# Five more places to yield in the recurrence streams of a hybrid layer, and two groups of copies in the other order

## The chip, the cores and the metric

One Trainium2 chip, one of its cores. The metric is device time in microseconds (us) of the whole launch. The engines are named as in the profile: PE (TensorE matmul) and PEld (its weight load), DVE (VectorE), ACT (ScalarE), POOL (GpSimd), SP (SyncE, which issues most transfers).

## The reference

One decoder layer on x of 2048 tokens and 1024 columns, float32. HGRN2 heads (four of 128) and RWKV-7 heads (eight of 64) run side by side on one input projection; one output projection and a ConvFFN follow.

```python
h = _rmsnorm(x, norm1_w[l])
proj = h @ w_in[l]
...
o_hg = _hgrn2_mixer(q_raw, f_raw, i_raw, g_raw, lower_bounds[l], hg_norm_w[l])
...
o_rw = _rwkv7_mixer(r, k, v, wd, ad, gd, rw_w0[l], rw_w2[l], rw_a0[l], rw_a2[l], rw_g2[l],
                    rw_k_k[l], rw_k_a[l], rw_r_k[l], rw_ln_w[l], rw_ln_b[l])
x = x + jnp.concatenate([o_hg, o_rw], axis=-1) @ w_out[l]
x = x + _conv_ffn(_rmsnorm(x, norm2_w[l]), w_up[l], conv_w[l], conv_b[l], w_down[l])
```

Inside the RWKV mixer the state follows S = S diag(w) + (S a) b^T + v k^T for each token, and y = S r. The kernel computes this by chunks of 64 tokens, which needs the inverse of a triangular 64 x 64 matrix for each chunk and head.

## The kernel before

The work has two stages. Stage 1 (to about 1350 us) makes the input projection, both mixers and the output projection; stage 2 is the ConvFFN and is not touched by the change. Stage 1 walks over four blocks of 512 tokens with three Python generators that emit instructions in turn:

- the dense stream: norm, turn, projection, and behind each block its output projection. Each float32 product is made of three matmuls of split operands (L265 to L267, with high and low halves that L242/L249 on ACT and L243/L250 on DVE make). `turn` (L436) transposes a block of x on PE, and eight ACT copies (xt) take the result from PSUM. The output projection of a block (L373 and below) loads pieces of w_out (woraw), splits them (L249, L250), multiplies, and adds the residual on DVE (L407).
- the RWKV stream, `rw_super`: eight steps, two for each block (each holds four of the eight heads). 
- the HGRN stream, `hg_unit`: sixteen units, four for each block, one head each.

The main loop at L1077 to L1086 advances the RWKV stream by one piece (up to its next `yield`), then the HGRN stream by one, then calls `fill(TICK)`, which advances the dense stream until pieces worth 2000 ns have been emitted. A `yield` in a mixer is therefore what puts dense matmuls between two dependent pieces of that mixer. A mixer that has to wait for its inputs yields `None` until the projection has made them. The emitted order is then set into an order for each engine by the framework, whose engines wait for each other by semaphores.

The pieces of one RWKV step that the change and the prediction speak of, in their order: KB and BV on DVE (L702); M from matmuls at L714; its blocks are copied out to E by a DMA; transposes and the copies UV and RHS on ACT (L120, the line of the helper `act`); lv at L763; the inverse of 32 x 32 blocks on DVE as 31 pairs L783 and L785, each reading what the one ahead wrote; TZ (L789), the transposed result; z at L802 and its ACT copy ZT; z2 at L815 and its ACT copy TTs; the product of the whole inverse with RHS at L828, whose result ACT copies to two places, M (three copies, the columns called Q) and UV (four copies). XH and xp follow: L848 reads UV and KBT, L862 reads M and KBT, and L865 and L868 on DVE take its results. Further down is a scan over eight chunks (L885, L887), L917 and the output copies.

One HGRN unit: hk at L926; transposed values VT; seven levels of scaling on DVE (L944 to L953) with matmuls at L969 and masks at L975; hk times Sf at L1004; the transposes KT at L1011, the state product at L1022 and its DVE scan (L1024); the norm of the output (osq) with matmul L1037; and L1042.

ACT's functions come from tables. `act` (L112 to L124) loads another table set where a function needs one that is not loaded (L116 in the profile): Exp and Ln share a set, Sigmoid and Tanh share one, Silu has its own; Copy, Square and Identity need none. So the number of loads depends on the order in which ACT's instructions are emitted.

Of the kernel before, what the change touches and what calls it, by code (L numbers as in the profile page):

```python
# [11 lines left out]
AF = mybir.ActivationFunctionType  # L12
# [52 lines left out]
def tile_layer(ctx, tc, consts, x, norm1_w, w_in, hg_lb_logits, hg_norm_w, rw_shift_mu, rw_w0, rw_w2,  # L65
# [46 lines left out]
    def act(out_, in_, func, **kw):  # L112

        want = tables.get(func)
        if want is not None and want != tab["now"]:
            pre = S.preload_act_table_set(want)  # L116
            for u_ in tab["uses"]:
                tc.add_manual_dep(pre.ins, u_.ins.name, NOSYNC, reason="table order")
            tab.update(now=want, pre=pre, uses=[])
        i_ = S.activation(out_, in_, func, **kw)  # L120
        if want is not None:
            tc.add_manual_dep(i_.ins, tab["pre"].ins.name, NOSYNC, reason="table order")
            tab["uses"].append(i_)
        return i_  # L124
# [144 lines left out]
    def phase1(c1):  # L269
# [354 lines left out]
        er0 = lambda e: 64 if e == 0 else 0  # L624

        def quads():

            return [(b, h, e, u) for b in range(4) for h in range(2) for e in range(2) for u in U]

        def col0(u, e):  # L630

            return er0(e) if u == 0 else 64 - er0(e)
# [5 lines left out]
        def rw_super(nb, s_):  # L638

            tl = stage[("tl", nb)]  # L640
            r, k, v = (stage.pop(("rkv", nb, s_, w)) for w in range(3))
            prs = (2 * s_, 2 * s_ + 1)
            pc = [slice(p * P, (p + 1) * P) for p in prs]

            def tile_(tag, shape, name):
                return rp.tile([P] + shape, F32, tag=tag, name=name)

            def bank2():
                return ps.tile([P, 2, BLK], F32, tag="rw", name="rw", bufs=2)
# [52 lines left out]
            V.tensor_mul(KB[:, :, 1:3, :], v16(c), v16(a))  # L702
            V.tensor_mul(BV, b1, v)
            yield

            M = tile_("M", [2, 2, 4, 2, P], "M")
            for j in range(2):
                for u in U:
                    s1 = bank2()
                    for i in range(4):  # L710
                        b, e = 2 * j + i // 2, i % 2
# [12 lines left out]
            for e in range(2):  # L724
                for q in range(2):
                    r0 = er0(e) + 32 * q
# [29 lines left out]
            act(RHS[0:64, :, :, 0:64], tpv[64:128], AF.Copy)  # L756
            done["rw1"] += 1
            yield

            lv = bank2()  # L760
            for b, h, e, u in quads():
                kr, c0, sl = 64 - er0(e), col0(u, e), (b * 2 + h) * 64
# [5 lines left out]
            for e in range(2):  # L768
                r0, c0 = er0(e), col0(1, e)
# [9 lines left out]
            for j in range(31):  # L779
# [6 lines left out]
                if j % 4 == 3:  # L786
                    yield
            TZ = tile_("XH", [16, 16, 2], "TZ")
            V.transpose(TZ.rearrange("p c m f -> p (c m f)"), Ti.rearrange("m t c -> m c t"))  # L789
            ZT = tile_("E", [16, 32], "ZT")  # L790
            TZm = TZ.rearrange("p c m f -> p m c f")
            for q in (1, 0):
                for e in range(2):
                    r0 = er0(e) + 32 * q
# [4 lines left out]
            for b, h, e, u in quads():  # L799
                r0 = er0(e)  # L800
                c0, sl = r0 + 32 - 32 * u, u * 256 + (b * 2 + h) * 32
                TE.matmul(z[c0:c0 + 32, 0, sl:sl + 32], M[r0:r0 + 32, e, u, b, h, 32:64],  # L802
                          TZm[r0:r0 + 32, u * 8 + b * 2 + h], start=True, stop=True, tile_position=(r0, c0))
            for u in U:
                for e in range(2):
                    r1 = er0(e) + 32
                    c0 = r1 - 32 * u
                    act(ZT[r1:r1 + 32, 8 * u:8 * u + 8],
                        z[c0:c0 + 32, 0, u * 256:u * 256 + 256].rearrange("p (s t) -> p s t", t=32), AF.Copy)
            yield  # L810
            z2 = bank2()
            for b, h, e, u in quads():
                r0 = er0(e)
                c0, sl = r0 + 32 * u, u * 256 + (b * 2 + h) * 32
# [3 lines left out]
            for u in U:  # L818
                for e in range(2):
                    r0 = er0(e)  # L820
                    c0 = r0 + 32 * u
# [4 lines left out]
            for b, h, e, u in quads():  # L826
                r0, c0, sl = er0(e), col0(u, e), ((b % 2) * 2 + h) * P
                TE.matmul(qus[u][c0:c0 + 64, b // 2, sl:sl + P], TTs[r0:r0 + 64, u * 8 + b * 2 + h, :],  # L828
                          RHS[r0:r0 + 64, 4 * u + b, h, :], start=True, stop=True, tile_position=(r0, c0))
            quv = [qus[u].rearrange("p j (b h t) -> p (j b) h t", h=2, t=P) for u in U]  # L830
            act(M[:, 0, 0, :, :, 0:64], quv[0][:, :, :, 0:64], AF.Copy)
            for e in range(2):
                r0, c0 = er0(e), col0(1, e)
                act(M[r0:r0 + 64, 0, 1, :, :, 0:64], quv[1][c0:c0 + 64, :, :, 0:64], AF.Copy)
            for u in U:
                for e in range(2):
                    r0, c0 = er0(e), col0(u, e)
                    act(UV[r0:r0 + 64, 4 * u:4 * u + 4, e, :].rearrange("p b (h t) -> p b h t", t=64),
                        quv[u][c0:c0 + 64, :, :, 64:128], AF.Copy)
            yield  # L840
            XH = tile_("XH", [2, 9, 64], "XH")
            V.tensor_copy(XH[:, :, 0, :], Xc[:, 2 * s_:2 * s_ + 2, :])
            xp = bank2()
            for u in U:
                for ch in range(8):
                    b, e = ch // 2, ch % 2
# [24 lines left out]
            for u in U:  # L871
                for ch in range(8):
                    b, e = ch // 2, ch % 2
# [5 lines left out]
            for ch in range(8):  # L879
                b, e = ch // 2, ch % 2  # L880
                cs_ = slice(ch * 64, ch * 64 + 64)
                for u in U:
                    for h in range(2):
                        hr = slice(h * 64, h * 64 + 64)
                        TE.matmul(xp[hr, u, cs_], M[hr, 1, u, b, e, 0:64], XH[hr, u, ch, :], start=False,  # L885
                                  stop=ch == 7, tile_position=(h * 64, h * 64), skip_group_check=True)
                V.tensor_mul(XH[:, :, ch + 1, :], xp[:, :, cs_], WC2[:, :, ch].broadcast_to([P, 2, 64]))  # L887
                yield
            V.tensor_copy(Xc[:, 2 * s_:2 * s_ + 2, :], XH[:, :, 8, :])
            for u in U:  # L890
                for ch in range(8):
                    cs_ = slice(ch * 64, ch * 64 + 64)
                    for h in range(2):
                        hr = slice(h * 64, h * 64 + 64)
                        TE.matmul(yp[hr, u, cs_], XH[hr, u, ch, :], RT[hr, u, ch, :], start=False, stop=ch == 7,
                                  tile_position=(h * 64, h * 64), skip_group_check=True)
# [26 lines left out]
        def hg_unit(nb, j):  # L923
# [79 lines left out]
            X = scaled(6)  # L1003
            V.tensor_mul(k, k, Sf)  # L1004
            V.tensor_mul(q, q, Pf)
            yield
            KT = rp.tile([P, 4, P], F32, tag="Sf", name="KT")
            tp = bank("hg")
            lp = bank("hg")
# [4 lines left out]
                          start=True, stop=True, tile_position=(0, 0))  # L1014
            act(KT, tp.rearrange("p (b t) -> p b t", t=P), AF.Copy)
            act(Af[0:64, :, 64:128], lp[0:64, 0:256].rearrange("p (b t) -> p b t", t=64), AF.Copy)
            yield
            SH = rp.tile([P, 5, P], F32, tag="SH", name="SH")
            V.tensor_copy(SH[:, 0, :], Sc[:, j, :])
            sps = bank("hg")  # L1020
# [26 lines left out]
        def rw_stream():  # L1047
            for n in range(2 * NBLK):
                while ready["rw"] <= n:
                    yield None  # L1050
                yield from rw_super(n // 2, n % 2)

        def hg_stream():
            for n in range(4 * NBLK):
                while ready["hg"] <= n:
                    yield None
                yield from hg_unit(n // 4, n % 4)
# [517 lines left out]
```

## Time and profile before

| | us |
|---|---|
| three runs | 2685.09, 2686.59, 2689.0 (median 2686.59) |
| the profiled execution, its own time | 2686.26 |
| its span in the profile | 2684.5 |
| granted clock of PE, mean | 0.994 |
| stage 1 of the span | 0 to about 1350 |
| first output projection (in stage 1) | 569.7 to 654.1 |
| second output projection | 917 to 1000 |

The span is the time from the first to the last recorded instruction; the execution's own time has some 1.8 us more around it. A group's row names line, engine, operation and tiles, then busy time and mean of one, and behind the second bar the idle time ahead of such instructions with what ended it. A row of the timeline gives start and length in us. A row of waits gives the engine and line that waited, the engine and tile that ended the wait, the sum in us, how often, and the longest.

### The profile page before, as it was taken

How to read it: one execution, taken by the hardware profiler on the slowest of the kernel's cores; microseconds unless marked ns; L12 is line 12 of the kernel's file. 1: busy time of each engine (PE TensorE's matmuls, PEld its weight loads, DVE VectorE, ACT ScalarE, POOL GpSimd, SP SyncE). 2: the span in 40 equal slices, each digit the busy share in tenths (PEclk: the TensorE clock that was granted, in tenths of full speed). 3: DMA queues.
4: the chain of work that ended last, by engine and by line, in shares of the span. 5: the costliest groups of instructions: out<-in, count | busy, mean ns of one | idle time of the engine just before them, and what ended most of it. 6: DMA issues, size and time to landing. Idle time of an engine off the chain costs nothing.

```text
span 2684.5 us, 47831 instructions
## 1 busy us (share of the span) xinstructions
PE 2614.7 (97%) x18059; PEld 2091.1 (78%) x18059; DVE 1929.6 (72%) x3705; ACT 1338.3 (50%) x2158; POOL 381.8 (14%) x684
## 2 busy tenths in 40 slices
PE   7999999999999999999999999999999999999998
PEld 5777777777777777778778888887888888788887
DVE  4867757576466764657578789988998888676556
ACT  4555442454544545433357665456555545445444
POOL 6433222212222123222100000000000000000000
PEclk9999999999999999999899999999999999999999
DMA  8654543355643556834584458756764463898665
GB/s 304 198 166 162 166 135 117 115 161 195 197 149 116 157 161 214 290 115 132 160 272 149 134 184 267 243 171 194 259 200 149 149 202 124 311 325 282 203 192 184
DMA packets 312828, 510.52 MB, mean 190 GB/s; under 512 B 46879, under 2 KB 143509, under 8 KB 312597
## 3 DMA queue, kind: packets, MB, share of 16 engines
q1 hardware_dynamic: 258225, 329.65, 37.2%
q0 software_dynamic: 54304, 177.80, 20.3%
q8 instruction: 142, 2.33, 0.4%
q14 instruction: 89, 0.73, 0.1%
q10 hardware_dynamic: 68, 0.02, 0.0%
HBM read 373.13 MB, written 134.22 MB: 189 GB/s over the span
## 4 chain that ended last, share of the span: by engine, by line
PE 74%; DVE 7%; DMA 6%; issue 6%; ACT 5%; POOL 1%; SPq 0%; DVEq 0%; POOLq 0%; ACTq 0%
PE pj L265 8%; PE pj L266 7%; PE pj L267 7%; PE ua L265 5%; PE ua L267 5%; PE ua L266 5%; PE da L266 3%; PE da L267 3%; PE da L265 3%; PE ud L266 2%; PE ud L265 2%; PE ud L267 2%; PE hg L969 2%; PE db L265 2%; PE db L266 2%
## 5 line engine op out<-in xcount | busy, mean ns | idle before, releaser
L265 PE MATMUL pj<-hh,wh 128*128 128x512 f32 x960 | 404.1, 421 | 4.5 <-ACT rkv L120 1.7
L266 PE MATMUL pj<-hl,wh 128*128 128x512 f32 x960 | 377.9, 394 | 0.0
L267 PE MATMUL pj<-hh,wl 128*128 128x512 f32 x960 | 377.7, 394 | 0.0
L265 PE MATMUL ua<-Bh,uwh 128*128 128x512 f32 x704 | 275.9, 392 | 1.0 <-ACT m L120 0.9
L267 PE MATMUL ua<-Bh,uwl 128*128 128x512 f32 x704 | 274.3, 390 | 0.0
L266 PE MATMUL ua<-Bl,uwh 128*128 128x512 f32 x704 | 274.1, 389 | 0.0
L265 PEld LDWEIGHTS pj<-hh,wh 128*128 128x128 f32 x960 | 181.2, 189 | 59.6 <-issue 14.0
L267 PEld LDWEIGHTS pj<-hh,wl 128*128 128x128 f32 x960 | 181.0, 189 | 40.1 <-issue 0.6
L266 PEld LDWEIGHTS pj<-hl,wh 128*128 128x128 f32 x960 | 181.5, 189 | 38.7 <-issue 5.9
L249 ACT CAST uwh<-uraw 128x512 fp32r<-128x512 f32 x220 | 135.1, 618 | 138.0 <-PE ua L266 63.2
L250 DVE TENSOR_TENSOR dal<-draw,dah 128x512 fp32r<-128x512 f32 x138 | 95.3, 690 | 113.1 <-ACT dah L249 113.0
L250 DVE TENSOR_TENSOR uwl<-uraw,uwh 128x512 fp32r<-128x512 f32 x220 | 147.3, 686 | 34.8 <-ACT uwh L249 34.8
L249 ACT CAST dah<-draw 128x512 fp32r<-128x512 f32 x138 | 85.8, 622 | 167.3 <-PE da L266 78.7
L265 PEld LDWEIGHTS ua<-Bh,uwh 128*128 128x128 f32 x704 | 132.2, 188 | 29.8 <-ACT m L120 2.4
L267 PEld LDWEIGHTS ua<-Bh,uwl 128*128 128x128 f32 x704 | 132.2, 188 | 28.1 <-DVE uwl L250 0.4
L266 PEld LDWEIGHTS ua<-Bl,uwh 128*128 128x128 f32 x704 | 132.2, 188 | 26.6
L265 PE MATMUL ud<-Bh,uwh 128*128 128x512 f32 x352 | 138.0, 392 | 0.0
L267 PE MATMUL ud<-Bh,uwl 128*128 128x512 f32 x352 | 137.0, 389 | 0.0
L266 PE MATMUL ud<-Bl,uwh 128*128 128x512 f32 x352 | 137.0, 389 | 0.0
L1445 POOL DMA_DIRECT2D gd<-y x2 | 1.1, 556 | 947.0 <-DVE y L1443 947.0
L266 PE MATMUL da<-dbl,dah 128*128 128x512 f32 x332 | 129.5, 390 | 1.1 <-DVE dbl L250 1.1
L267 PE MATMUL da<-dbh,dal 128*128 128x512 f32 x332 | 129.2, 389 | 0.0
(570 smaller groups left out, 6199.2 us busy)
## 6 DMA issues: line engine op xcount, KB each, us to landing
uraw<-in_w_up_dram SPq DMA_DIRECT2D x176, 256.0 KB, 3.3
woraw<-in_w_out_dram POOLq DMA_DIRECT2D x96, 256.0 KB, 3.4
br<-gd SPq DMA_DIRECT2D x88, 256.0 KB, 4.1
draw<-Sg SPq DMA_DIRECT2D x88, 256.0 KB, 3.0
draw<-Tw SPq DMA_DIRECT2D x88, 256.0 KB, 3.5
gd<-y SPq DMA_DIRECT2D x86, 256.0 KB, 2.8
Sg<-br SPq DMA_DIRECT2D x72, 256.0 KB, 2.6
xt<-x1d SPq DMA_DIRECT2D x32, 512.0 KB, 5.9
```

The costliest lines, as they stand in the source:

```text
L249: S.copy(hi, src)
L250: V.tensor_sub(lo, src, hi.bitcast(F32))
L265: TE.matmul(acc, lh, rh, start=first, stop=False, skip_group_check=skip)
L266: TE.matmul(acc, lh, rl, start=False, stop=False, skip_group_check=skip)
L267: TE.matmul(acc, ll, rh, start=False, stop=last, skip_group_check=skip)
L969: TE.matmul(o, kt[:, t0:t0 + 64], qs, start=True, stop=True, tile_position=(0, e * 64))
L1445: (dma if end is None else nc.gpsimd.dma_start)(gd_[2 * h + b][fb * P:(fb + 1) * P, :], ys[0][:, b * BLK:(b + 1) * BLK])
```

## The change

Four `yield`s are added to each of the first six RWKV steps: ahead of M (L714), ahead of lv (L763), ahead of z2 (L815) and ahead of XH and xp (L848). In the HGRN units up to number 13 the `yield` ahead of KT (L1011) and the one ahead of SH (L1022) become two each. In all eight RWKV steps the four UV copies come ahead of the three M copies.

```diff
             r, k, v = (stage.pop(("rkv", nb, s_, w)) for w in range(3))
+            more = range(1 if 2 * nb + s_ < 6 else 0)
...
             V.tensor_mul(BV, b1, v)
             yield
+            for _ in more:
+                yield
...
             done["rw1"] += 1
             yield
+            for _ in more:
+                yield
...
             yield
+            for _ in more:
+                yield
             z2 = bank2()
...
+            for u in U:
+                for e in range(2):
+                    r0, c0 = er0(e), col0(u, e)
+                    act(UV[r0:r0 + 64, 4 * u:4 * u + 4, e, :].rearrange("p b (h t) -> p b h t", t=64),
+                        quv[u][c0:c0 + 64, :, :, 64:128], AF.Copy)
             act(M[:, 0, 0, :, :, 0:64], quv[0][:, :, :, 0:64], AF.Copy)
             for e in range(2):
                 r0, c0 = er0(e), col0(1, e)
                 act(M[r0:r0 + 64, 0, 1, :, :, 0:64], quv[1][c0:c0 + 64, :, :, 0:64], AF.Copy)
-            for u in U:
-                for e in range(2):
-                    r0, c0 = er0(e), col0(u, e)
-                    act(UV[r0:r0 + 64, 4 * u:4 * u + 4, e, :].rearrange("p b (h t) -> p b h t", t=64),
-                        quv[u][c0:c0 + 64, :, :, 64:128], AF.Copy)
-            yield
+            yield
+            for _ in more:
+                yield
...
             V.tensor_mul(q, q, Pf)
-            yield
+            for _ in range(2 if 4 * nb + j < 14 else 1):
+                yield
...
-            yield
+            for _ in range(2 if 4 * nb + j < 14 else 1):
+                yield
```

The first place is on ACT, behind the product with the inverse in the first RWKV step. Before:

```order
L120 ACTIVATE TTs<-rw 32x8x32 x4
L249 CAST wh<-wraw 128x512
L120 ACTIVATE rkv_1692<-pj,omu 128x512
L120 ACTIVATE hX<-hk 128x256
L120 ACTIVATE M<-rw 128x8x64
L120 ACTIVATE M<-rw 64x8x64 x2
L120 ACTIVATE UV<-rw 64x4x128 x4
L120 ACTIVATE VT<-hg 128x512
```

Now:

```order
L120 ACTIVATE VT<-hg 128x512
L249 CAST wh<-wraw 128x512
L120 ACTIVATE rkv_1610<-pj,omu 128x512
L120 ACTIVATE hX<-hk 128x256
L120 ACTIVATE UV<-rw 64x4x128 x4
L120 ACTIVATE M<-rw 128x8x64
L120 ACTIVATE M<-rw 64x8x64 x2
```

UV has moved ahead of M. On PE, 10 dense matmuls and four transposes stood between L828 and L848 here; now it is 18 dense matmuls (L828 is L835 in the changed file, L848 is L857).

The second place is on DVE, in the chain of the fourth RWKV step (step 3), around its twentieth pair (etmp of 126 elements; L783 and L785 are L788 and L790 in the changed file). Before:

```order
L783 TENSOR_TENSOR etmp<-E,Ti 128x126
L785 TENSOR_TENSOR Ti<-Ti,etmp 128x18x7
L783 TENSOR_TENSOR etmp<-E,Ti 128x136
L785 TENSOR_TENSOR Ti<-Ti,etmp 128x17x8
L783 TENSOR_TENSOR etmp<-E,Ti 128x128
```

Now:

```order
L250 TENSOR_TENSOR wl<-woraw,wh 128x512
L788 TENSOR_TENSOR etmp<-E,Ti 128x120
L407 TENSOR_TENSOR xh<-pj,xh 128x512
L790 TENSOR_TENSOR Ti<-Ti,etmp 128x20x6
L407 TENSOR_TENSOR xh<-pj,xh 128x512
L788 TENSOR_TENSOR etmp<-E,Ti 128x133
L996 TENSOR_TENSOR A<-hg,cst 128x256
L790 TENSOR_TENSOR Ti<-Ti,etmp 128x19x7
L984 COPY_PREDICATED A<-cst,hg 128x128
L788 TENSOR_TENSOR etmp<-E,Ti 128x126
```

The chain has moved into the first output projection: between its pairs stand pieces of that projection (L250, L407) and levels of an HGRN unit.

The third place is on ACT, at the turn of the second block, where the xt copies are. Before:

```order
L116 ACT_TABLE_LOAD
L120 ACTIVATE W<-mk 128x16x64
L120 ACTIVATE ai<-mk 128x1024
L249 CAST wh<-wraw 128x512
L120 ACTIVATE mk<-mk 128x1024 x2
L116 ACT_TABLE_LOAD
L120 ACTIVATE hf<-pj 128x512
L249 CAST wh<-wraw 128x512
L120 ACTIVATE xt<-pj 128x4x128 x2
L120 ACTIVATE Sf<-hf 128x256
L120 ACTIVATE xt<-pj 128x4x128 x6
```

Now:

```order
L120 ACTIVATE xt<-pj 128x4x128 x2
L120 ACTIVATE mk<-ai,oka,vt 128x512
L116 ACT_TABLE_LOAD
L120 ACTIVATE xt<-pj 128x4x128 x2
L120 ACTIVATE W<-mk 128x16x64
L120 ACTIVATE xt<-pj 128x4x128 x2
L120 ACTIVATE ai<-mk 128x1024
L120 ACTIVATE xt<-pj 128x4x128 x2
L120 ACTIVATE mk<-mk 128x1024
```

The RWKV step's load and its W, ai and mk have moved from ahead of the eight xt copies to between them. (W, ai, mk are the decay and its inverse; hf and Sf belong to an HGRN unit.) In all, 67 table loads stand in ACT's order where 53 stood.

More of the change, by code (lines that the diff above doesn't have):

```diff
@@ L830, in rw_super @@
             quv = [qus[u].rearrange("p j (b h t) -> p (j b) h t", h=2, t=P) for u in U]
-            act(M[:, 0, 0, :, :, 0:64], quv[0][:, :, :, 0:64], AF.Copy)
-            for e in range(2):
-                r0, c0 = er0(e), col0(1, e)
-                act(M[r0:r0 + 64, 0, 1, :, :, 0:64], quv[1][c0:c0 + 64, :, :, 0:64], AF.Copy)
             for u in U:
@@ L839, in rw_super @@
                         quv[u][c0:c0 + 64, :, :, 64:128], AF.Copy)
+            act(M[:, 0, 0, :, :, 0:64], quv[0][:, :, :, 0:64], AF.Copy)
+            for e in range(2):
+                r0, c0 = er0(e), col0(1, e)
+                act(M[r0:r0 + 64, 0, 1, :, :, 0:64], quv[1][c0:c0 + 64, :, :, 0:64], AF.Copy)
             yield
+            for _ in more:
+                yield
             XH = tile_("XH", [2, 9, 64], "XH")
```

## The prediction

> **What bounds the kernel now.** I read the page's first lines, then the chain of waits, then busy time by stretch.
>
> ```profile
> span 2684.5 us, 47831 instructions
> PE 2614.7 (97%) x18059; PEld 2091.1 (78%) x18059; DVE 1929.6 (72%) x3705; ACT 1338.3 (50%) x2158; POOL 381.8 (14%) x684
> ...
> PE 74%; DVE 7%; DMA 6%; issue 6%; ACT 5%; POOL 1%; SPq 0%; DVEq 0%; POOLq 0%; ACTq 0%
> ```
>
> The stretches (length, then busy time and count of PE, PEld, DVE, ACT and POOL, the granted clock, the DMA share, GB/s):
>
> ```profile
> 0.00:1350.00 1350.00, 1298.85 (x12257) 1007.54 (x12257) 872.79 (x2110) 628.04 (x1016) 367.60 (x658) 0.99 0.52 170
> 1350.00:2684.50 1334.50, 1315.83 (x5802) 1083.52 (x5802) 1056.80 (x1596) 710.27 (x1143) 14.23 (x27) 1.00 0.64 211
> ```
>
> PE is busy 97% of the span. The change adds and removes no arithmetic, so it can move only PE's waits, and only in the first stage, which the diff touches (to about 1350 us). There PE idles 1350 - 1298.85 = 51 us by the window's count. The waits of PE inside the stage, by who ended them, are these (column order: engine, line waited at, who came last: us in all, times, longest):
>
> ```profile
> PE vps L154 <- DMA rows<-in_hg_lb_logits_dram: 10.8, 1, 10.8
> PE rw L848 <- ACT UV L120: 6.5, 6, 2.0
> PE pj L265 <- ACT hh L242: 6.4, 5, 2.2
> ...
> PE pj L265 <- DVE xh L407: 2.6, 4, 1.0
> PE hg L1011 <- DVE hk L1004: 2.4, 1, 2.4
> PE rw L862 <- DVE AR L868: 2.2, 1, 2.2
> PE pj L436 <- ACT xt L120: 1.7, 6, 0.6
> ...
> PE rw L815 <- ACT ZT L120: 1.5, 3, 0.8
> ...
> PE rw L802 <- DVE TZ L789: 1.0, 3, 0.4
> ...
> PE hg L1022 <- ACT KT L120: 0.8, 2, 0.4
> ...
> PE rw L714 <- DVE KB L702: 0.7, 2, 0.5
> ```
>
> The first is the wait for the first load and stays. The places where a yield is added are L714, L815, L848, L1011 and L1022 (and L763, whose wait is 0.2 us). They hold 6.5 + 2.4 + 1.5 + 0.8 + 0.7 = 11.9 us, 0.44% of the run. That is the size of the prize. The dense stream fills the rest: its matmuls follow each other at 0.23 us.
>
> ```profile
> 137.24 0.39 PE L266 MATMUL pj<-hl,wh 128*128 128x512 f32 x1
> 137.47 0.39 PE L267 MATMUL pj<-hh,wl 128*128 128x512 f32 x1
> 137.70 0.40 PE L265 MATMUL pj<-hh,wh 128*128 128x512 f32 x1
> ```
>
> **The gains.** One yield is one round of the loop, in which `fill` emits dense work until 2000 ns of credit are spent: three groups of three matmuls, 9 x 0.229 = 2.06 us of PE. At the worst place, the first step's L848, the rows are:
>
> ```profile
> 151.21 1.80 ACT L120 ACTIVATE M<-rw 128x512 f32<-128x512 f32 x3
> 153.03 2.43 ACT L120 ACTIVATE UV<-rw 64x512 f32<-64x512 f32 x4
> ...
> 154.27 2.27 PE L848 MATMUL rw<-UV,KBT 128*64 128x64 f32 x64 [2.02 <-ACT UV L120]
> 156.47 0.69 PE L862 MATMUL rw<-M 64*64 64x64 f32 x32
> ```
>
> ACT makes M first (1.80 us) and UV after it; L848 reads UV, while M is read only by L862, 2.2 us behind. With UV first, UV is there 1.80 us earlier, in all eight steps. The pause adds 2.06 us of PE work ahead of L848 in steps 0 to 5. Worst case 2.02 - 1.80 = 0.2 is left without the pause, nothing with it: **-6.5 us**. M now comes out 1.80 us after UV, and L848's matmuls, which start on UV, take 2.2 us (154.27 to 156.47): they hide it, so the swap has no price. Without that cover it would be 1.80 us a step.
>
> The others, each against its row. L815: two waits in step 2 sum to most of 1.5 and fall to a pause; step 7 has none and keeps its 0.4: **-1.1**. L714: 0.5 and 0.2 are both below 2.06: **-0.7**. L1022: 2 x 0.4, of which I count one half: **-0.4**. L1011: 2.4 against 2.06: **-2.2**. L802 and L862 get no yield; the order around them shifts with the rest. There I take **-0.5** of 1.0 and **-1.2** of 2.2, bounds nothing and all, since their cause (DVE held up by a DMA) can fall anywhere. Sum of the gains **-12.6**, bounds -8 (UV and half the others) and -15.
>
> **The losses.** A pause has no price where PE fills it. But the rounds in which a step waits for its inputs are used up: the total stays the same and later pieces slide against the dense blocks. Three places are worse in the new order.
>
> *ACT at the turns.* Before a new block of 512 tokens PE transposes x (L436) and ACT evicts it (xt).
>
> ```profile
> 221.47 0.60 ACT L120 ACTIVATE hf<-pj 128x512 f32<-128x512 f32 x1
> 221.97 0.61 ACT L249 CAST wh<-wraw 128x512 fp32r<-128x512 f32 x1
> 222.47 1.09 ACT L120 ACTIVATE xt<-pj 128x512 f32<-128x512 f32 x2
> ...
> 226.89 1.09 ACT L120 ACTIVATE xt<-pj 128x512 f32<-128x512 f32 x2 [0.26 <-PE pj L436]
> ...
> L116 ACT ACT_TABLE_LOAD x44 | 56.5, 1283 | 1.5 <-PEq L1560 0.7
> ```
>
> The eight evictions take 5.5 us, with nothing but one small copy between, and PE waits 1.1 + 0.2 there. In the new order of ACT a table load and the step's W, ai and mk stand among them (front part, third place). The first turn gets mk 0.6, the load 1.28, W 1.07, ai 1.04 and mk 1.08: 5.1 us, less the small copy (0.4) = 4.6 of ACT time. PE has only transposes there, so between nothing and 4.6 is lost: I take **+3.2**. The third turn has the same pieces: **+3.2**. The second has one load only, before which PE waited 0.4: nothing more. In all there are 14 more table loads in the stage, 44 to 58 (18 us of an engine half idle); those elsewhere I count at **+0.7** (the osq chain ahead of L1037 in the first output block).
>
> [...]
>
> ```profile
> 1129.83 1.56 ACT L120 ACTIVATE TTs<-rw 32x256 f32<-32x256 f32 x4
> 1131.41 1.28 ACT L116 ACT_TABLE_LOAD   x1
> 1132.70 0.69 ACT L120 ACTIVATE osq<-hg,eps 128x512 f32<-128x512 f32 x1
> ```
>
> From the end of TTs (1131.39) to the start of osq it is 1.31 us, so a switch costs its load alone.
>
> *DVE in the first output block.* Step 3's triangular inverse is 31 pairs of L783 and L785, one after the other. The window from its first L783 to L802, which reads its result:
>
> ```profile
> 545.27:578.48 33.21, 31.67 (x248) 25.41 (x248) 30.63 (x108) 13.72 (x25) 6.09 (x11) 1.00 0.50 153
> ...
> L785 DVE TENSOR_TENSOR Ti<-Ti,etmp 128x126 f32<-128x126 f32 (+22 forms) x248 | 62.8, 253 | 3.6
> L783 DVE TENSOR_TENSOR etmp<-E,Ti 128x126 f32<-128x126 f32 (+22 forms) x248 | 62.2, 251 | 10.3 <-DMA E<-Ed 6.9
> ...
> L250 DVE TENSOR_TENSOR wl<-woraw,wh 128x512 fp32r<-128x512 f32 x96 | 65.6, 687 | 43.7 <-ACT wh L249 42.9
> ...
> L407 DVE TENSOR_TENSOR xh<-pj,xh 128x512 f32<-128x512 f32 x24 | 16.1, 685 | 0.7 <-PE pj L267 0.7
> ```
>
> Of 33.21 us DVE was busy 30.63, and the result came just in time. Now most of the chain lies behind the start of that block, which brings its own DVE work: 18 L250 and 6 L407 between the pairs, where four and none stood. By the order DVE issues 124 instructions from the block's first L407 to TZ: 30 x 0.251 + 31 x 0.253 (the chain) + 18 x 0.687 + 6 x 0.685 + the HGRN levels (25 at 0.42, 6 at 0.34) and a few more, 49.1 us. Neighbours overlap by some 0.08 us (556.32 + 0.28 against 556.52 in the timeline rows below), so 49.1 - 124 x 0.075 = 39.8.
>
> ```profile
> 556.32 0.28 DVE L783 TENSOR_TENSOR etmp<-E,Ti 128x120 f32<-128x120 f32 x1
> 556.52 0.42 DVE L950 TENSOR_TENSOR hX<-hk,Sf 128x256 f32<-128x256 f32 x1
> 556.85 0.28 DVE L785 TENSOR_TENSOR Ti<-Ti,etmp 128x120 f32<-128x120 f32 x1
> ```
>
> PE has between the same points 111 dense matmuls (25.4 us) and 7.4 us of others: 32.8. PE waits the difference, 7.0 us. The block's old waits (about 4.5 us, the L407 ones among them) are partly the same lateness, so I add **+4.0**, bounds nothing and +8.5. Step 5 meets the second output block in the same way with 10 L250 instead of 3: its DVE sum, counted in the same way, grows from 34.9 to 40.7 us, by 4.1 on the path, most of it covered: **+1.3**, bounds nothing and +4.1.
>
> Losses: 3.2 + 3.2 + 0.7 + 4.0 + 1.3 = **+12.4**. Net -0.2 on the profiled execution, whose own time is 2686.26 (span 2684.5 and 1.8 around it), so 2686.1; the median of the runs lies 0.3 above it: **2686.4 us**. What a measurement can tell from no change is about 0.2%, 5.4 us.
>
> **The rivals.** *Faster: the losses are hidden.* The gains are read off rows, the losses are built from an order. If DVE's lateness in the output blocks is the lateness that was already paid (4.5 us there before) and a turn costs half of what I say, -12.6 + 3.2 = -9.4: **2677**. For it: the DVE was idle elsewhere in the block, and the pairs may slide. Against: 49 us of DVE work in 33 us of PE.
>
> *Slower: DVE becomes the bound in the output blocks.* Place: step 3's chain in the first, step 5's in the second; price +8.5 and +4.1 instead of 4.0 and 1.3, since none of the old waits goes away. That is 2686.4 + 7.3 = **2694**. It decides once the chain's end runs more than about 9 us behind PE in the first block. For it: the new L250s stand between the pairs in DVE's order, and behind each pair the next waits. Against: L250 and L407 feed PE too, so while DVE works on them PE is served.
>
> *The pauses do only part of what they say.* Each engine's order is rebuilt after emission, and for step 3 the PE work between L828 and L848, counted from the order, stays (2.57 to 2.73 us). UV's 6.5 come from the swap alone; if the other places, 6.1 by my sum, give half, it is 2686.4 + 3.0 = **2689.4**, inside 0.2%.
>
> **How the numbers follow.** The forecast, gains and losses cancel (the third rival included, which ends inside 0.2% too): 0.40. Faster: 0.33. Slower: 0.27. The likeliest one's own range is 2681 to 2692; both others hold too much to leave out, so the range is **2676 to 2696**, from all gains with the bounds' lower losses to the slower rival and 2 more. Faster by over 0.2%: 0.33; within: 0.40; slower: 0.27.
>
> **What would show it.** In the new profile's waits: L848 on UV below 0.5 us in all (gain), L1011 on hk and L815 on ZT near nothing in steps 0 to 5. Table loads 58 in the stage. At the first and third turn L436 waits of 3 to 5 us on xt. In the first output block a wait at L802 on TZ, or at L265 on L407 or L250, of 7 us or more in sum. Wrong would be: no new wait at the turns and no more than 5 us in the block (then 2677), or UV's wait still there. The clock of 0.99 and the second stage's 1334.5 us should not move; if they do, nothing here explains it.

## The result, and the profile after

The change is slower: 2704.35 us in the median of six runs against 2685.84 us, a ratio of 1.0072 with a 95% interval of 1.0061 to 1.0082, or 16 to 22 us. The profiled execution took 2702.77 us, its span 2700.9. Lines below L641 have moved down by 1 to 11 in it (L802 is L807, L815 is L822, L848 is L857, L862 is L871).

The first lines of the page after, and its chain of waits:

```profile
span 2700.9 us, 47824 instructions
...
PE 2618.8 (97%) x18059; PEld 2092.0 (77%) x18059; DVE 1929.5 (71%) x3705; ACT 1355.7 (50%) x2172; POOL 379.9 (14%) x684
...
PE 65%; DVE 11%; issue 9%; DMA 7%; ACT 4%; POOL 2%; SPq 0%; DVEq 0%; POOLq 0%; ACTq 0%
```

Work by stretch after: stage 1, then the first and the second output projection (length, then PE, PEld, DVE, ACT, POOL busy, the granted clock, the DMA share, GB/s).

```profile
0.00:1366.00 1366.00, 1302.22 (x12255) 1009.73 (x12256) 872.52 (x2108) 646.68 (x1031) 365.20 (x657) 0.99 0.51 168
...
553.00:644.00 91.00, 82.58 (x795) 61.57 (x792) 69.78 (x182) 49.51 (x84) 16.56 (x31) 0.98 0.52 157
922.00:1009.00 87.00, 77.28 (x872) 57.05 (x870) 63.42 (x152) 39.23 (x70) 15.34 (x29) 0.96 0.49 151
```

The same two blocks before:

```profile
569.00:655.00 86.00, 81.76 (x941) 59.27 (x940) 65.92 (x146) 46.11 (x79) 15.20 (x29) 1.00 0.52 159
917.00:1001.00 84.00, 80.37 (x935) 59.01 (x935) 63.05 (x134) 45.69 (x77) 14.81 (x28) 1.00 0.51 161
```

All of the loss is in stage 1, which ends near 1366 us instead of 1350. PE's idle time there is 1366 - 1302.22 = 63.8 us, where it was 51.2: 12.6 more. PE's busy time for the same instructions grew by 1302.22 - 1298.85 = 3.4 us, with more of them at a lower clock, as shown below. The two add up to the 16 us by which the stage is longer. Of the idle time 4.2 us more lie in the first output block (8.4 against 4.2) and 6.1 more in the second (9.7 against 3.6).

The waits of PE in stage 1 after, as in the prediction:

```profile
PE pj L265 <- ACT hh L242: 10.4, 9, 2.6
PE rw L807 <- DVE TZ L794: 5.0, 6, 1.6
PE pj L436 <- ACT xt L120: 4.2, 5, 2.0
PE pj L265 <- ACT wh L249: 3.1, 3, 2.2
...
PE rw L822 <- ACT ZT L120: 2.9, 2, 2.5
PE pj L266 <- DVE wl L250: 2.8, 5, 1.0
PE rw L871 <- DVE AR L877: 2.0, 2, 1.1
...
PE rw L822 <- issue: 1.6, 1, 1.6
PE hg L1021 <- DVE Ti L790: 1.4, 1, 1.4
...
PE rw L857 <- ACT M L120: 0.5, 3, 0.2
```

The wait on UV is gone: of 6.5 us at this line 0.5 are left, on M. In its place TZ is waited for (1.0 to 5.0), ZT (1.5 to 2.9), hh (6.4 to 10.4), wh and wl. The "issue" row at L822 is a wait of 1.6 us ahead of the last matmul of its group, at 954.03, for which the profile shows no cause.

The clock is the second part. The trace's clock records hold these stretches at 0.50 (start and length in us; the last one before lies just behind stage 1):

```
before   437.0 3.41   1112.9 3.41   1276.7 6.83   1310.8 6.83   1355.2 3.41
after    222.1 6.83    618.0 3.41    952.5 6.83   1140.3 10.24  1293.9 6.83   1328.0 6.83
```

In stage 1 that is 20.5 us before and 41 us after. The last two of the change repeat two of before (1276.7 and 1310.8) 17 us later; the four ahead of them are new, and those at 437.0 and 1112.9 are gone. Over all runs of the first comparison the mean granted clock of the change was 0.988 to 0.991, that of the kernel before in the later runs 0.992 to 0.996. The lengths listed are all multiples of 3.41 us, and the starts lie on a grid of the same step: in each of these two executions they are whole multiples of 3.413 us apart (from 222.1 to 618.0 are 116). The longest single wait ahead of the stretch at 222 was 2.0 us.

### The profile page after: what moved, and what is told of

Same layout as the page of the kernel before. It is cut to its first block, busy times and chain, and to the rows that moved or that the text cites. A ratio compares the mean times of both kernels' runs of the same rounds, so it can differ in the third digit from the quotient of the medians.

```text
span 2700.9 us, 47824 instructions
## 1 busy us (share of the span) xinstructions
PE 2618.8 (97%) x18059; PEld 2092.0 (77%) x18059; DVE 1929.5 (71%) x3705; ACT 1355.7 (50%) x2172; POOL 379.9 (14%) x684
## 4 chain that ended last, share of the span: by engine, by line
PE 65%; DVE 11%; issue 9%; DMA 7%; ACT 4%; POOL 2%; SPq 0%; DVEq 0%; POOLq 0%; ACTq 0%
PE pj L265 7%; PE pj L266 6%; PE pj L267 6%; PE ua L265 4%; PE ua L267 4%; PE ua L266 4%; PE da L266 3%; PE da L267 3%; PE da L265 3%; PE ud L266 2%; PE ud L265 2%; PE ud L267 2%; PE db L265 2%; PE db L266 2%; PE db L267 2%
## 5 line engine op out<-in xcount | busy, mean ns | idle before, releaser
L250 DVE TENSOR_TENSOR dal<-draw,dah 128x512 fp32r<-128x512 f32 x138 | 95.3, 691 | 112.2 <-ACT dah L249 111.8
L250 DVE TENSOR_TENSOR uwl<-uraw,uwh 128x512 fp32r<-128x512 f32 x220 | 147.6, 688 | 34.4 <-ACT uwh L249 34.2
```

Of the source, the lines that this page charges most:

```text
L250: V.tensor_sub(lo, src, hi.bitcast(F32))
```

## The experiments

Every experiment starts from the kernel before or from the change. Times are medians; a ratio is to the kernel before on the same chip. The profile of each is of one execution; PE's idle and busy time of stage 1, where given, is counted to the end of the stage's last dense matmul (before: 51.0 idle, 1298.8 busy).

**The parts of the change.** `e1_uv_first` is the kernel before with the swap alone:

```diff
+            (four UV copies)
             (three M copies)
-            (four UV copies)
             yield
```

> Only the swap of the copies, no pauses; ACT's order has the same table loads as before (none among the xt copies) and every step starts where it did. If the loss of the change comes from the pauses (they shift RWKV steps into the turns and the output blocks), this one keeps the gain alone: the 6.5 us of waits of L848 on UV fall to under 1 us, and the time is 4 to 8 us below before, 2678 to 2682. If the swap itself hurts (M, which is late by 1.80 us now, delays L862), L862 waits on M and the time is that of before or above.

2684.26 us, ratio 0.9990 (0.9978 to 1.0002): no gain that can be told. Its timeline at the first step shows why, ACT's copies first, then PE:

```profile
148.67 2.40 ACT L120 ACTIVATE UV<-rw 64x512 f32<-64x512 f32 x4
151.10 1.81 ACT L120 ACTIVATE M<-rw 128x512 f32<-128x512 f32 x3
...
151.75 2.08 PE L848 MATMUL rw<-UV,KBT 128*64 128x64 f32 x64 [1.34 <-ACT M L120]
```

UV was done at 151.07, yet L848 started at 151.75, just behind the first of the three M copies (151.10 + 0.60). L848 does not read M. But its result xp comes from `bank2`, a pool of two buffers, and both hold the product that the seven copies read. The first is free only when M's first copy is through. The sum of L848's waits stayed:

```profile
PE rw L848 <- ACT M L120: 6.6, 7, 1.3
```

The pauses alone, in one stream each:

```diff
e2   4 x "for _ in more: yield" in rw_super; hg_unit and copies as before
e3   2 x "for _ in range(2 if 4 * nb + j < 14 else 1): yield" in hg_unit; rw_super as before
e4   the change with the three M copies ahead of the four UV copies again
```

> Only the four pauses in the first six RWKV steps, M ahead of UV as before, single yields in the HGRN units. Eight table loads more than before, three turns with W, ai and mk or a load among the xt copies. Theory 1, the RWKV pauses carry the loss: 12 to 20 us above before (2698 to 2706), with half-clock stretches near the turns. Theory 2, the loss comes from RWKV and HGRN pauses together (14 more loads): only 4 to 10 us above.

2702.13 us, ratio 1.0062 (1.0046 to 1.0077): theory 1's range. Its sign did not come: no stretch at half clock begins near a turn (they begin at 302, 958, 1132, 1296 and 1326), and the stage has 27.3 us of it, where the change has 41. The stage is 17.1 us longer all the same, 14.0 of them idle time of PE and 3.2 busy time.

> Only the double yields in 14 HGRN units. No table load more than before and none among the xt copies. Theory 1: within 4 us of before (2682 to 2690), the wait of L1011 on hk gone, nothing else new. Theory 2: 4 to 10 us above before.

2686.29 us, ratio 1.0000 (0.9988 to 1.0012). Waits moved (L857, which is L848, waited 4.9 us for UV at one place), but the idle time of the stage is 52.5 us, 1.5 more than before. This execution has 37.5 us at half clock in stage 1, nearly as much as the change, with 3.0 us more of busy time, and took 2686.41 us.

> The change with M ahead of UV again, all pauses kept. The pauses alone cover UV in steps 0 to 5, so only steps 6 and 7 get their UV waits back (1.03 and 0.19 us): 1 to 2 us above the whole change, about 2705. If the swap is what helps with the pauses in place too, 5 us or more above it, 2709.

2701.40 us, ratio 1.0055 (1.0038 to 1.0073), not to be told from the whole change. So the RWKV pauses carry the loss; the HGRN pauses and the swap do nothing in sum.

**Which pauses.** The change with the pauses in the second or the first step of a block only:

```diff
-            more = range(1 if 2 * nb + s_ < 6 else 0)
+            more = range(1 if 2 * nb + s_ < 6 and s_ == 1 else 0)     # e5
+            more = range(1 if 2 * nb + s_ < 6 and s_ == 0 else 0)     # e6
```

> The whole change, but the RWKV pauses only in steps 1, 3 and 5, the second step of a block. Behind these the stream waits for the next block's projection anyway, so no later step starts late; steps 1, 3 and 5 start where they did. Theory 1 (the loss is that a pause in the first step of a block makes the second step start late, so that its table load, W, ai and mk fall among the xt copies and its inverse into the output block): the turns are clean at blocks 1 and 3, and the time is 2682 to 2690. Theory 2 (any RWKV pause costs, wherever it is): half of the loss stays, 2692 to 2697.

2696.99 us, ratio 1.0047 (1.0033 to 1.0061): theory 2's range. Theory 1 falls in this form: the first turn is clean, but the odd steps alone lose some 12 us. PE idles 85.00 - 77.15 = 7.9 us in the first output block (4.2 before), and hh is what it waits for most.

```profile
564.00:649.00 85.00, 77.15 (x853) 55.98 (x852) 65.31 (x162) 39.22 (x70) 15.53 (x29) 0.98 0.50 154
```

```profile
PE pj L265 <- ACT hh L242: 4.8, 5, 1.4
```

Over the whole stage the idle time of this execution is that of before (51.3 us), since other waits became shorter. What makes the stage 7.1 us longer is busy time, 6.9 us more, with 30.7 us at half clock.

> The whole change, but the RWKV pauses only in steps 0, 2 and 4, the first step of a block. Steps 1, 3 and 5 start late as in the change. Theory 1: nearly the whole loss is here, 2697 to 2705. Theory 2: half of it, 2692 to 2697.

2699.84 us, ratio 1.0050 (1.0031 to 1.0069): inside theory 1's range. Each half alone costs more than half of the loss, about the same, so neither theory has both runs.

**Lateness without pauses.** Plain yields ahead of steps 1, 3 and 5:

```diff
                 while ready["rw"] <= n:
                     yield None
+                if n in (1, 3, 5):
+                    for _ in range(4):
+                        yield
                 yield from rw_super(n // 2, n % 2)
```

> The kernel before with four plain yields at the start of RWKV steps 1, 3 and 5, none inside a step, and the copies as before: a pure shift of these steps by four rounds, as the pauses of an even step cause. Theory 1 (the lateness of the second step of a block is what costs, through the turns and the output blocks): it loses as the pauses in the even steps did, 10 to 16 us above before (2695 to 2701). Theory 2 (a pause inside a step costs where it stands): no more than 4 us above before (below 2690).

2697.90 us, ratio 1.0051 (1.0036 to 1.0066). No pause stands inside a step, no copy has moved, and it costs what the even steps' pauses cost. For these the lateness is the cause; for the odd steps' own pauses (`e5`) no run separates it. In the profiled execution (2703.44 us) PE's idle time in stage 1 is 10.6 us above before: 2.4 of it in the first turn, 1.5 and 2.4 in the first two output blocks, and the rest elsewhere, 2.6 of it in a longer wait on hk at 1124. Its first turn (waits of PE, 216 to 230 us):

```profile
PE pj L436 <- ACT xt L120: 2.3, 2, 2.0
PE rw L693 <- DVE BV L691: 1.0, 1, 1.0
PE rw L675 <- ACT ai L120: 0.4, 1, 0.4
```

The converse keeps all pauses and gives four rounds back inside the even steps:

```diff
                 V.tensor_mul(XH[:, :, ch + 1, :], xp[:, :, cs_], ...)
-                yield
+                if ch % 2 or s_ or 2 * nb + s_ >= 6:
+                    yield
```

> The whole change, but in steps 0, 2 and 4 the scan over eight chunks yields only behind every second chunk, four rounds fewer: the step keeps its four pauses and the second step of the block starts in its old round. Theory 1: the loss of the even steps is gone and that of the odd steps is left: 5 us or more below the change (below 2699), with no load or W among the xt copies of the turns of blocks 1 and 3 and no wait of L436 above 0.6 us there. Theory 2: as the change, 2701 to 2708, or worse, since the scan has less to hide behind.

2692.10 us, ratio 1.0033 (1.0020 to 1.0046): by the ratios some 10 us below the change, as theory 1 had it. 7 us of loss are left, with the odd steps' pauses. At the first turn the one row of L436 left is this:

```profile
PE pj L436 <- ACT xt L120: 0.8, 2, 0.6
```

One pause instead of four (the swap with the pause ahead of XH and xp alone):

> The swap of the copies and one pause only, the one ahead of XH and xp, in steps 0 to 5; the other three places and the HGRN units as before. One round of shift instead of four. The waits of L848 in steps 0 to 5 go (5.5 us). Theory 1: the shift of one round still puts W, ai and mk of step 1 or 3 among the xt copies of the first or second turn, so 2 to 8 us of the gain are eaten: 2682 to 2690. Theory 2: one pause of four costs a quarter of the loss and saves 5 us: 2683 to 2687.

2688.41 us, ratio 1.0011 (1.0001 to 1.0022): at the edge of what can be told from before, and no gain. L851, which is L848 here, still waits 2.5 us on M, and L436 at the turns 5.1 us on xt, where it was 1.7 before: in these waits even one round of lateness is paid for.

```profile
PE pj L436 <- ACT xt L120: 5.1, 7, 1.3
PE rw L851 <- ACT M L120: 2.5, 5, 1.2
```

The number of table loads does not explain these times: stage 1 has 44 before, 50 in `e5`, `e11` and `e12`, 52 in `e2` and `e10` and 58 in the change, while `e11` loses 3 us and `e5` 12.

**The turn and the clock.** ACT at the first turn of the change:

```profile
217.16 1.09 ACT L120 ACTIVATE xt<-pj 128x512 f32<-128x512 f32 x2
218.12 0.84 ACT L120 ACTIVATE mk<-ai,oka,vt 128x512 f32<-128x512 f32 x1
218.97 1.28 ACT L116 ACT_TABLE_LOAD   x1
220.27 1.08 ACT L120 ACTIVATE xt<-pj 128x512 f32<-128x512 f32 x2
221.24 1.06 ACT L120 ACTIVATE W<-mk 128x1024 f32<-128x1024 f32 x1
222.19 1.09 ACT L120 ACTIVATE xt<-pj 128x512 f32<-128x512 f32 x2
223.14 1.08 ACT L120 ACTIVATE ai<-mk 128x1024 f32<-128x1024 f32 x1
225.87 0.60 ACT L120 ACTIVATE xt<-pj 128x512 f32<-128x512 f32 x1 [1.65 <-PE pj L436]
```

In the last row ACT waits for PE, which runs at half clock by then (0.50 from 222.1 us). A version of the change makes PE do each transpose of this turn twice:

```diff
-                for i in range(4):
+                for i in [i_ for _ in range(2 if nb == 1 else 1) for i_ in range(4)]:
                     TE.transpose(tp[:, i * P:(i + 1) * P], ...)
```

> The whole change with each transpose of the first turn made twice (32 transposes more, about 3.5 us of PE work without use). In the change PE waits 0.4, 2.0 and 0.8 us around this turn and runs at half clock from 222 to 229 us. Theory 1 (the waits put PE at half clock, which costs again): with PE busy through the waits the half-clock stretch is gone, and the dense matmuls behind the turn come no more than 1 us later than in the change although 3.5 us of work were added. Theory 2 (the clock doesn't follow the waits): the stretch stays and the matmuls come 2 to 3.5 us later.

One run, 2697.01 us. Of the change, PE's busy time and clock in two stretches (first and seventh number behind the times):

```profile
220.00:224.00 4.00, 2.24 (x10) 1.42 (x11) 4.00 (x7) 3.99 (x7) 0.00 (x0) 0.76 0.00 0
224.00:228.00 4.00, 4.00 (x13) 2.52 (x11) 3.67 (x5) 2.10 (x4) 0.00 (x0) 0.50 0.02 4
```

And with the transposes doubled:

```profile
220.00:224.00 4.00, 3.95 (x30) 3.13 (x30) 4.00 (x7) 4.00 (x6) 0.00 (x0) 1.00 0.02 4
224.00:228.00 4.00, 3.71 (x21) 2.93 (x19) 3.96 (x7) 3.80 (x7) 0.00 (x0) 1.00 0.00 0
```

With 32 useless transposes the clock stays at 1.00, and a dense matmul behind the turn comes 22.8 us after one ahead of it (210.6 to 233.4), where the same two are 24.2 us apart in the change (211.6 to 235.8): 1.5 us less with 3.5 us of work more. The other work between the two matmuls is the same, but its order moved with the filler: L676 comes in two pairs, and one pair of L694 stands behind the turn. So the 1.5 us belong to filler and order together. (In that run a stretch of 6.83 us at half clock follows at 299.9, where the change has none.)

The link between the waits and half clock has more behind it than this one run. Five executions have this first turn's waits in the same form, 3.7 us in sum with one of 2.0: the change, `e4`, `e6`, `e10` and `e13`. All five drop to half clock there, at 221.8 to 224.9. In the others no wait of that turn is longer than 1.3 us, and none drops, `e11` with 3.4 us of waits on xt included.

The table load alone, in the kernel before:

```diff
                 act(t_[:, :, k * P:(k + 1) * P], ..., AF.Copy)
+                if nb == 1 and k == 2:
+                    act(dummy, t_[:, 0, k * P:k * P + 1], AF.Exp)
```

> The kernel before, with one small Exp activation behind the third xt copy of the first turn, which puts two table loads into that turn (2.6 us of ACT) and changes nothing else. Theory 1 (a wait costs twice, once itself and once through the half clock that follows it): the waits of L436 at this turn grow from 1.3 to about 3.2 us, and a half-clock stretch of 3.41 or 6.83 us follows near 225, where the trace of before has none, so that the dense matmuls behind the turn come 3.5 to 5.5 us later in all. Theory 2 (a wait costs itself): 1.5 to 2 us later, no half-clock stretch.

One run, 2690.76 us. The turn's waits came to this, 0.6 us more than before, and no half-clock stretch followed:

```profile
PE pj L438 <- ACT xt L120: 1.9, 3, 1.3
```

The dense matmul behind the turn came 0.6 us later. Theory 2 is nearer, and its size was too large: two loads by themselves cost PE little. That in the change it is the load together with W, ai and mk is the reading of the rows above, and no run separates them. This execution's time says nothing beyond that: its dense matmuls also followed each other at 0.233 us throughout stage 1, where it was 0.229 before, and why is not known.

**The copies by halves.** From the bank that e1 found: free the first buffer early.

```diff
             for u in U:
                 for e in range(2):
                     act(UV[... 4 * u:4 * u + 4 ...], quv[u][...], AF.Copy)
+                if u == 0:
+                    act(M[:, 0, 0, :, :, 0:64], quv[0][:, :, :, 0:64], AF.Copy)
+            (the two M copies of the second half)
```

> The kernel before, with the copies by halves: UV of the first half, M of the first half, UV of the second half, M of the second. With all UV first, L848 waited 1.34 us three times, by the records on M: its result xp takes the bank that the copies of the first half read, so it needs M's first copy too. Theory 1 (the bank is what L848 waits for): both needs of the first half are met after about 1.9 us of copies instead of 3.1 (all UV first) or 4.2 (before), the waits of L848 in steps 0 to 6 fall from 6.5 us to under 2, and the time is 4 to 6 us below before. Theory 2 (L848 waits for all copies of M): waits as before, 2685 to 2688.

2681.18 us, ratio 0.9986 (0.9974 to 0.9998): 3.4 us below before, a little less than expected.

```profile
153.01 1.20 ACT L120 ACTIVATE UV<-rw 64x512 f32<-64x512 f32 x2
154.11 0.58 ACT L120 ACTIVATE M<-rw 128x512 f32<-128x512 f32 x1
154.71 1.21 ACT L120 ACTIVATE UV<-rw 64x512 f32<-64x512 f32 x2
...
154.74 2.27 PE L849 MATMUL rw<-UV,KBT 128*64 128x64 f32 x64 [1.03 <-ACT M L120]
```

L849 (L848) starts 0.05 us behind the end of M's first copy, while the second half of UV is still being copied: the bank is shown. The waits of L849 that are left are 3.8 us instead of under 2, and L863 (L862) waits 0.9 us on M.

**The output blocks and the store.** One edit apart from the pauses: osq shares hk's one buffer, so the next HGRN unit's first DVE instruction waits for osq's store (8.4 us in stage 1 of the change, 7.4 before).

```diff
-            sq = rp.tile([P, BLK], F32, tag="hk", name="osq")
+            sq = rp.tile([P, BLK], F32, tag="hX", name="osq", bufs=3)
```

> The whole change, with osq in one of the three hX buffers instead of hk's only one, so that the first DVE instruction of the next HGRN unit (hk) no longer waits for the store of osq. In the change it waits 8.4 us in sum over the first stage, and the pairs of the inverse, L250 and L407 stand behind it in DVE's order. Theory A (the output blocks lose through the amount of DVE work): these 8.4 us go, but the waits of PE in the two blocks stay above 7 us each and the time falls by 3 us at most (2700 and above). Theory B (they lose through that store): the second block's 9.7 us of waits fall below 6, and the time falls by 5 us or more (below 2699).

2697.19 us, ratio 1.0042 (1.0025 to 1.0058), some 8 us below the change. Neither theory has it whole. The idle time of PE in the first output block stays (8.5 us), and in the second it falls from 9.7 to 7.3 us, not below 6: at most 2.4 us of these blocks' loss go with the store. More went near the end of the stage, where the idle time falls from 6.9 to 3.6 us and both stretches at half clock are gone. The first two output blocks here, then the last 107 us of the stage in the change and here:

```profile
559.00:647.00 88.00, 79.47 (x782) 59.37 (x783) 69.28 (x182) 49.20 (x84) 15.53 (x29) 1.00 0.54 162
927.00:1011.00 84.00, 76.68 (x882) 57.01 (x881) 62.77 (x152) 38.72 (x70) 15.01 (x28) 0.98 0.49 158
```

```profile
1259.00:1366.00 107.00, 100.12 (x1103) 79.18 (x1100) 76.76 (x199) 47.65 (x86) 17.39 (x32) 0.94 0.43 141
1255.00:1362.00 107.00, 103.38 (x1214) 79.58 (x1212) 79.10 (x211) 51.64 (x92) 19.06 (x36) 1.00 0.46 151
```

> The kernel before with the same edit of osq's buffer. Its hk waited 7.4 us for the store, 3.8 of them at 1140 us, which PE paid for with 2.2 us at L862. Theory B: that wait of L862 goes, 2 to 4 us below before (2681 to 2683). Theory A: within 2 us of before.

2677.07 us, ratio 0.9965 (0.9952 to 0.9977), more than twice what theory B had. The group of hk in stage 1 of this kernel, where the last figure is DVE's idle time ahead of it (before it was 7.6, of which 7.4 on the store):

```profile
L926 DVE TENSOR_SCALAR hk<-hf 128x512 f32<-128x512 f32 x16 | 7.0, 438 | 0.8 <-PE hg L1011 0.7
```

Only one stretch of 3.41 us at half clock is left in its stage 1. The stage is 11.4 us shorter: 7.7 us of idle time and 3.7 of busy time went. How much of either follows from the store and how much from the clock is not told apart.

> The kernel before with the copies by halves (UV, M of the first half, then of the second) and osq's buffer changed. The two edits touch different waits, so their gains should add: 3.5 us of the halves and 0 (theory A) to 4 us (theory B) of the buffer: 2677 to 2682.

2672.09 us, ratio 0.9947 (0.9928 to 0.9967): 15 us below the 2687.59 us of the kernel before on that chip and the fastest of all, without any pause. It lies below the expected range because the buffer alone brought 10.5 us; with the 3.4 of the halves the gains add up within the noise.

## Why the prediction was wrong

It forecast gains and losses that cancel, 2686.4 us, and the time was 2704. Point by point, from the profile after:

| term | predicted | measured in PE's waits |
|---|---|---|
| UV at L848 | -6.5 | -6.0 |
| ZT at L815 | -1.1 | +1.4, and +1.6 without a cause shown |
| TZ at L802 | -0.5 | +4.0 |
| hk at L1011 | -2.2 | -0.5 (with Ti) |
| AR at L862 | -1.2 | -0.2 |
| KB at L714, KT at L1022 | -1.1 | -1.1 |
| first turn, third turn | +3.2, +3.2 | +2.4, +2.8 |
| osq ahead of L1037 | +0.7 | +0.5 |
| first output block | +4.0 | +4.2 |
| second output block | +1.3 | +6.1 |
| a lower clock | none | +3.4 of busy time |

(The blocks' idle time contains some of the TZ, ZT and hk waits, so the column does not add up to 16.)

Right were the size of UV's wait, the turns within a microsecond, and the size of the first output block; the 58 table loads came too (44 before). In that block the place was only partly right: no wait on TZ came at L802, none on L407, and 2.5 us on wl; the rest was hh (2.3), an HGRN unit's Ti (1.4) and wh (0.9). The number there is in part luck. That a step's lateness costs, and in part in the turns and output blocks, was right too: e10 shows it without any pause.

Three steps failed.

1. The gains at the other waits. The prediction took -5.0 us at L1011, L862, L815 and L802, and they came out at +4.7, or +6.3 with the wait at L815 that has no cause shown. It priced the waits of before and did not ask which other DVE or ACT result would be late next once the steps slide. The waits of before did go in part (ZT in step 2), but ZT is now waited for in step 6, which has no pause (2.5), and TZ in steps 1, 2 and 6 (1.5, 0.8, 1.6). TZ is the end of the inverse's chain, and between the chain's pairs stand other DVE instructions. The waits were exchanged, not removed.
2. The second output block: "most of it covered: +1.3". Its DVE sum was worked out to be 4.1 us longer on the path; the block's idle time grew by 6.1. With that price the rival called slower had the right place and too small a sum (2694). The kind of wait was wrong too: PE waits there for ACT's hh (4.4 us, 1.8 before) and wh (2.2, 0.3 before), and behind some of these waits ACT itself waited for loads, which the prediction had no price for. The largest such rows:

```profile
923.92 0.62 ACT L242 CAST hh<-oraw 128x512 fp32r<-128x512 f32 x1 [3.00 <-DMA oraw<-oT]
946.10 0.62 ACT L249 CAST wh<-woraw 128x512 fp32r<-128x512 f32 x1 [4.42 <-DMA woraw<-in_w_out_dram]
```

Before, the longest such wait in the block was 1.4 us. What made these loads late, DVE's work that frees their buffers or something else, is open; the osq store accounts for at most 2.4 us (e13).

3. The clock. It was read (0.99) and put at nothing. New waits ahead of 222, 618, 952 and 1140 us were followed by 3.41 to 10.24 us at half clock; the third turn's were not. At the first turn it followed these waits in five executions of five, and in e7, with PE busy through most of them, the clock stayed at 1.00. It is the smaller part of the loss, 3.4 us of busy time: e2 loses as much with 27.3 us at half clock, and e3 has 37.5 us of it and no loss in its median. Only in e5's execution is busy time the larger part.

That the swap saves 1.80 us a step and has no price was wrong in its reason too. The cover named (M behind UV hidden under L848) does not exist, since L848 does not start before M's first copy frees its bank (0.05 us behind that copy in e1 and in e9). In the change the pause hid this; alone (e1) the swap is worth nothing that can be told. So the -6.0 at UV came from the pauses: in `e4`, which has them without the swap, L857's wait on UV is 0.5 us too. The forecast's size was right, the swap's share of it was not.

Two bounds do not follow from the prediction's own terms: UV and half of the other gains make -9.5, not -8, and all gains with the lowest losses (0.7) would end near 2672, not 2676. Neither changes the outcome, which lies above the range.

The pauses do what they say at UV and KB. What they cost lies mostly elsewhere: four rounds later the second step of a block meets the turn and the output projection, whose work sits between its pieces in the orders of ACT and DVE.

## What to carry to other kernels

A pause in one of several interleaved streams was not made free here by the other work that its engine has (lateness alone, e10, cost 13 us). It moves everything behind it in that stream against the others; look at what the moved pieces land on, before counting the wait that they leave. Where a consumer waits for a copy, look also for the buffer that its own result will take. And before adding pauses, look for two tiles that share one buffer while one of them is still being stored: untying osq from hk brought 10 us, where twenty-four pauses in the RWKV steps alone cost 15 (e2).

## What the runs showed of the hardware

Behind a few waits close together (in the change 0.6, 0.4 and 2.0 us within 6 us) TensorE's granted clock was 0.50 for 3.41 or 6.83 us, in five executions of five. What wait it takes is not shown: `e8_load_in_turn` has a stretch of 3.41 us at 155.8 behind a single wait of 1.9 us, where the kernel before has none behind 2.0. In the kernel before and in the change all starts of the execution lie on one grid of 3.413 us. Why like waits end differently is not shown.

In one turn, with 32 useless transposes in the waits and the order that came with them (e7, one run), the clock stayed at 1.00 and the way through the turn was 1.5 us shorter than in the change.

The clock goes with the time of single runs of one kernel, which spread from 2678 to 2694 us: the later runs of the kernel before with a mean granted clock of 0.995 have a median of 2683.8 us, those with 0.993 one of 2687.8.

Half clock cost less than half of its length here: `e3_hg_pauses` has 17 us more of it in stage 1 than the kernel before, with 3.0 us more of busy time and 1.5 us more of idle time (one execution of each).
